# Latent attention with keys on partitions: scores computed transposed, row maxima from the high parts only, fp32 value products in two column halves

## Chip, cores, metric

One Trainium2 chip, one core. The metric is the device time of one execution in microseconds, lower is better; the time before is the median of three runs.

## The reference, cut to what matters

The kernel is one encoder layer: adaLN, an attention mixer with two head groups, an output projection, then a routed mixture of 16 experts. The change is in the first head group, the latent attention (eight heads, 1024 positions, 96 columns of q and k, 64 of v):

```python
def mla_attention(q, k, v):
    B, S, H, Dq = q.shape
    nblk = S // Q_BLOCK
    scale = Dq ** -0.5
    qb = q.reshape(B, nblk, Q_BLOCK, H, Dq).transpose(1, 0, 2, 3, 4)

    def one_block(q_blk):
        s = jnp.einsum('bqhd,bkhd->bhqk', q_blk, k).astype(jnp.float32) * scale
        p = jax.nn.softmax(s, axis=-1).astype(v.dtype)
        return jnp.einsum('bhqk,bkhd->bqhd', p, v)

    o = lax.map(one_block, qb)
    return o.transpose(1, 0, 2, 3, 4).reshape(B, S, H, v.shape[-1])
```

## The kernel before

Everything is fp32. Where a plain fp32 product would be slow the kernel splits an operand into a high part, rounded to the type fp32r, and a low part, the rest (`split`, L82: the cast on ScalarE, the subtraction on VectorE), and adds three fp32r products, high x high, high x low and low x high.

The stages follow each other: adaLN and the input norm; the input projections (the latent q, k and v go to DRAM as `qd`, `kd`, `vd`; `kv_out`, L500, stores v through `vsplit`, L426, already as high and low part); the dilated attention (L668 to L837); the latent attention (L884 to L963); the output projection with the router (L1000 on); the experts (L1425 on). Instructions are placed on each engine's queue by a planner that may move one ahead of another in the text where its inputs and buffers allow it; an engine then works through its queue in order.

In the latent attention `load_head` (L585) brings a head's q, k and v, `prep_head` (L596) transposes 512 positions of q or k on TensorE and splits them. One step of the loop at L937 is one block of 128 queries. `mscore` (L616) puts queries on partitions: six products of 512 columns fill a 128x1024 block `big`, VectorE takes the maximum of each row, and `mexpo` (L640) lets ScalarE compute the exponentials with that maximum as its bias, and their sum. Two steps later `transp` (L898) transposes the exponentials on TensorE, eight blocks of 128x128, and splits them into `pth` and `ptl`. For every two blocks `pv` (L910) adds 16 products: the stationary side holds v's high and low parts beside each other (`k1h`), the moving side is `pth` or `ptl`; two halves of the result are added afterwards. The reciprocals of the sums go to DRAM and come back repeated over 64 partitions (`rows`), and GpSimd multiplies (L929).

The dilated attention has its own `score` (L707), `weights` (L746, a row of reciprocals stored and read back) and `pv` (L760), whose fp32 value products use the two column halves of the array (`tile_position=(0, 64 * e)`); their line is L770. A plain fp32 product shows in the trace as two records.

Of the kernel before, what the change touches and what calls it, by code (L numbers as in the profile page):

```python
# [13 lines left out]
F32 = mybir.dt.float32  # L14
F32R = mybir.dt.float32r
# [27 lines left out]
MS, ME = (1, 2), (2, 3)  # L43

ADV, AV, LATE = (2, 4, 6), 7, 6

KP, XD, WB, TW = 4, (1, 3, 5, 7), 4, 4

# [5 lines left out]
def block_kernel(ctx: ExitStack, tc: tile.TileContext, A: dict, out: bass.AP, dbg=None):  # L54
# [34 lines left out]
    vd = scratch("vd", [S, MH * 2 * VD])  # L89
# [336 lines left out]
    def vsplit(t, src, dst):  # L426

        vv = wk.tile([P, 8, 2, 64], F32R, name="vv")
        split(vv[:, :, 0], vv[:, :, 1], src)
        nc.sync.dma_start(dst[t * P:(t + 1) * P, :], vv.bitcast(F32).rearrange("p h z d -> p (h z d)"))  # L430
# [69 lines left out]
    def kv_out(t, got):  # L500
# [5 lines left out]
        vsplit(t, uv[:, :, ND:], vd)  # L506
# [78 lines left out]
    def load_head(h):  # L585
        e = h % 2
        q = qk_tile(f"k2h{e}", F32, NT * QD).rearrange("p (j c) -> p j c", c=QD)
        k = qk_tile(f"k2l{e}", F32, NT * QD).rearrange("p (j c) -> p j c", c=QD)
        v = qk_tile(f"k1h{e}", F32R, NT * 2 * VD).rearrange("p (j c) -> p j c", c=2 * VD)
        for eng, dst, src, n in ((nc.sync, k, kd, QD), (nc.sync, q, qd, QD), (nc.gpsimd, v, vd, 2 * VD)):  # L590
            eng.dma_start(dst, src[:, h * n:(h + 1) * n].rearrange("(j p) c -> p j c", p=P))
        loads[h] = (q, k, v)
# [3 lines left out]
    def prep_head(h, n, z):  # L596

        q, k, v = loads[h]
        if h not in hs:
            hs[h] = {x: (qk_tile(f"{y}h{h % 2}", F32R), qk_tile(f"{y}l{h % 2}", F32R))  # L600
                     for x, y in (("q", "q1"), ("k", "q2"))}
            hs[h]["v"] = v
# [10 lines left out]
    sc, den, rows, last_exp = {}, {}, {}, [None]  # L613
    drow = scratch("drow", [MH, S])

    def mscore(h, t, early=False):  # L616
        T = hs[h]
        qh, ql = T["q"]
        kh, kl = T["k"]
        qs = slice(t * P, (t + 1) * P)  # L620
        if early:
            ps = [mid(), mid()]
        else:
            b = big()
            ps = [b[:, 0:512], b[:, 512:1024]]
        for a, b_, first, last in ((qh, kh, True, False), (qh, kl, False, False), (ql, kh, False, True)):
            for z in range(2):
                nc.tensor.matmul(ps[z], a[:QD, qs], b_[:QD, z * 512:(z + 1) * 512], start=first, stop=last)  # L628
        if early:
            mx = const.tile([P, 3], F32, name="mxe", bufs=2)  # L630
            for z in range(2):
                nc.vector.tensor_reduce(mx[:, z:z + 1], ps[z], axis=AX.X, op=ALU.max)
# [977 lines left out]
```

## Time and profile before

| what | value |
|---|---|
| median of three runs | 1394.82 us (1392.77 to 1396.35) |
| the profiled execution | 1390.52 us |
| its span | 1388.0 us |
| mean granted TensorE clock | 0.988 of full speed |
| busy: TensorE, VectorE, ScalarE, GpSimd | 95%, 80%, 64%, 14% |

The span goes from the first to the last instruction of the profiled execution, whose own time lies 2.5 us above it; the median of the timed runs is 4.3 us higher. A matmul's record covers its whole way through the array, so records overlap, and the rate is read from the distance of their starts. "x6" behind a shape counts the instructions of a merged row.

### The profile page before, as it was taken

The numbers are of one execution on the slowest core, as the hardware profiler recorded it, in microseconds if no ns is written. First come the engines' busy times: TensorE is split into PE (matmuls) and PEld (weight loads), VectorE is DVE, ScalarE is ACT, GpSimd is POOL, SyncE is SP. The second block draws the span as 40 slices with busy tenths as digits, with TensorE's granted clock in tenths as the row PEclk, the third lists the DMA queues.
The fourth block names the chain that finished last, engine by engine and source line by source line (L and its number), as shares of the span: only waits on it lengthen the run. The fifth ranks groups of instructions, "written<-read, shape, count | busy, mean of one in ns | idle before, by whom it ended". The sixth has DMA issues, their size and how long they took to land.

```text
span 1388.0 us, 21350 instructions
## 1 busy us (share of the span) xinstructions
PE 1324.7 (95%) x7710; PEld 1076.0 (78%) x7710; DVE 1104.5 (80%) x2088; ACT 888.8 (64%) x1421; POOL 191.0 (14%) x230
## 2 busy tenths in 40 slices
PE   4999999999999999999998599999999999999997
PEld 3787788965557999997887478888888888887774
DVE  5764567466657888888477889999999999988887
ACT  5622124255546777777432488888888888878874
POOL 1021011110005101002220121111111111410010
PEclk9999999999999999999999699999999999999999
DMA  9785567254225242112544899999999999999934
GB/s 272 198 284 184 164 230 260 68 153 123 73 57 168 47 80 58 24 24 83 192 166 153 332 345 337 391 393 389 393 391 393 395 390 389 394 364 360 358 105 199
DMA packets 162704, 325.36 MB, mean 234 GB/s; under 512 B 41499, under 2 KB 84571, under 8 KB 162598
## 3 DMA queue, kind: packets, MB, share of 16 engines
q1 hardware_dynamic: 149398, 301.97, 60.5%
q0 software_dynamic: 13200, 22.02, 6.7%
q8 instruction: 60, 0.98, 0.3%
q14 instruction: 46, 0.38, 0.1%
HBM read 286.66 MB, written 37.31 MB: 233 GB/s over the span
## 4 chain that ended last, share of the span: by engine, by line
PE 88%; DVE 6%; ACT 2%; DMA 2%; issue 1%; SPq 0%; DVEq 0%; ACTq 0%
PE big L1354 23%; PE big L1405 12%; PE big L628 6%; PE big L1045 6%; PE mid L916 4%; PE mid L907 4%; PE mid L78 4%; PE mid L80 3%; PE mid L79 3%; PE big L725 2%; PE mid L743 2%; PE mid L1328 2%; PE mid L770 2%; PE big L720 1%; PE big L1369 1%; PE big L78 1%
## 5 line engine op out<-in xcount | busy, mean ns | idle before, releaser
L1314 DVE TENSOR_TENSOR mwl<-mraw,mwh 128x1024 fp32r<-128x1024 f32 x384 | 450.2, 1221 | 28.9 <-ACT mwh L1312 25.3
L1312 ACT CAST mwh<-mraw 128x1024 fp32r<-128x1024 f32 x384 | 391.6, 1062 | 54.1 <-PE big L1354 44.8
L1354 PE MATMUL big<-mwh,xeh 128*128 128x512 f32 x480 | 149.5, 393 | 0.2 <-ACT mwh L1312 0.2
L1354 PE MATMUL big<-mwl,xeh 128*128 128x512 f32 x480 | 149.2, 392 | 0.5 <-DVE mwl L1314 0.5
L1354 PE MATMUL big<-mwh,xel 128*128 128x512 f32 x480 | 147.9, 390 | 0.0
L1354 PEld LDWEIGHTS big<-mwl,xeh 128*128 128x128 f32 x480 | 89.3, 188 | 20.5 <-DVE mwl L1314 2.1
L1354 PEld LDWEIGHTS big<-mwh,xel 128*128 128x128 f32 x480 | 90.0, 188 | 19.1
L1354 PEld LDWEIGHTS big<-mwh,xeh 128*128 128x128 f32 x480 | 88.9, 188 | 19.8 <-ACT xeh L83 0.8
L78 PE MATMUL mid<-wh,hTh 128*128 128x512 f32 (+2 forms) x264 | 94.7, 359 | 0.0
L79 PE MATMUL mid<-wl,hTh 128*128 128x512 f32 (+2 forms) x264 | 93.2, 353 | 0.0
L80 PE MATMUL mid<-wh,hTl 128*128 128x512 f32 (+2 forms) x264 | 93.2, 353 | 0.0
L83 ACT CAST pth<-mid 128x512 fp32r<-128x512 f32 x128 | 68.7, 589 | 34.7 <-PE mid L907 34.2
L84 DVE TENSOR_TENSOR ptl<-mid,pth 128x512 fp32r<-128x512 f32 x128 | 85.3, 682 | 1.0 <-ACT pth L83 0.3
L1321 POOL DMA_INDIRECT xe<-h2d,ix x16 | 37.3, 2333 | 352.9 <-DVE xel L84 330.6
L1405 PE MATMUL big<-mwl,hTh 128*128 128x512 f32 x256 | 80.7, 395 | 2.6 <-DVE mwl L1314 2.5
L1405 PE MATMUL big<-mwh,hTh 128*128 128x512 f32 x256 | 81.4, 398 | 0.4 <-ACT mwh L1312 0.4
L636 DVE TENSOR_REDUCE mx<-big 128x1 f32<-128x1024 f32 x62 | 75.6, 1219 | 6.5 <-PE big L628 6.1
L1405 PE MATMUL big<-mwh,hTl 128*128 128x512 f32 x256 | 79.4, 390 | 0.0
L734 ACT ACTIVATE P<-P,mx 128x512 f32<-128x512 f32 x64 | 45.7, 716 | 43.3 <-DVE mx L730 43.3
L916 PE MATMUL mid<-pth,k1h 128*128 128x256 f32 x256 | 64.9, 292 | 0.5 <-DVE mx L637 0.5
L1334 ACT ACTIVATE xe<-mid,cols 128x128 f32<-128x128 f32 x128 | 48.9, 471 | 21.1 <-PE mid L1328 21.0
L916 PE MATMUL mid<-ptl,k1h 128*128 128x256 f32 x256 | 62.3, 282 | 0.0
(369 smaller groups left out, 2791.1 us busy)
## 6 DMA issues: line engine op xcount, KB each, us to landing
mraw<-in_w_gate_dram SPq DMA_DIRECT2D x64, 1024.0 KB
mraw<-in_w_up_dram SPq DMA_DIRECT2D x63, 1024.0 KB
mraw<-in_w_down_dram SPq DMA_DIRECT2D x63, 1024.0 KB
wada<-in_w_ada_dram SPq DMA_DIRECT2D x48, 512.0 KB
x<-in_x_dram SPq DMA_DIRECT2D x16, 512.0 KB
raw<-in_w_in_dram SPq DMA_DIRECT2D x12, 512.0 KB
vd<-vv SPq DMA_DIRECT2D x8, 512.0 KB
k1h<-vd POOLq DMA_DIRECT2D x8, 512.0 KB, 7.0
```

Of the source, the lines that this page charges most:

```text
L78: nc.tensor.matmul(o, xh, wh, start=start, stop=False, **kw)
L79: nc.tensor.matmul(o, xh, wl, start=False, stop=False, **kw)
L80: nc.tensor.matmul(o, xl, wh, start=False, stop=stop, **kw)
L84: return nc.vector.tensor_tensor(l, src, h.bitcast(F32), op=ALU.subtract)
L628: nc.tensor.matmul(ps[z], a[:QD, qs], b_[:QD, z * 512:(z + 1) * 512], start=first, stop=last)
L636: nc.vector.tensor_reduce(mx[:, 0:1], b, axis=AX.X, op=ALU.max)
L916: nc.tensor.matmul(op[:, 0:256], V[:, k], pt[:, k], start=(k == 0 and i == 0), stop=(k == NT - 1 and i == 1))
L1045: lastmm[0] = nc.tensor.matmul(ps[z], a[k], w[k][:, z * 512:(z + 1) * 512], start=(first and i == 0), stop=(last and i == KT - 1))
L1312: high[0] = nc.scalar.copy(h[j], raw[:, j])
L1314: low[0] = nc.vector.tensor_tensor(l[j], raw[:, j], h[j].bitcast(F32), op=ALU.subtract)
L1354: nc.tensor.matmul(o[:, zs], a[:, k], w[i][j][:, zs], start=(k == 0 and a is xh and i == 0), stop=(k == KT - 1 and a is xl))
L1405: nc.tensor.matmul(yp[:, zs], a[:, k], w[i][j][:, zs], start=(k == 0 and a is th and i == 0), stop=(k == KT - 1 and a is tl))
```

## The change

- `vout` takes the place of `vsplit`: v is stored in fp32, once, so `vd` and its load are half as large. `load_head` loads only q and k, into one buffer each (`k2h0`, `k2l0`); v is loaded by a function of its own.
- `maxpass`: for a block of 128 queries, the product of the high parts alone, over all keys, and its row maxima on VectorE. `maxrow`: one product brings the negated maxima of four blocks to four partitions, and VectorE writes them, each in its own block's columns and zero elsewhere, as rows 96 to 99 of the high part of q; the same rows of the high part of k hold ones.
- `score`: keys are on partitions now. 128 keys by 512 queries in three products; the first has 100 rows of contraction, so the maxima are subtracted in it. ScalarE's exponential goes straight from PSUM to a ring of 13 buffers. Nothing is transposed after it.
- `accum` adds the exponentials of the key blocks on VectorE; `dens` sums over partitions with eight fp32 products against a column of ones; `denrow` transposes the reciprocals, stores them and reads them back repeated.
- `pv`: for each block of 128 keys two fp32 products, 512 queries each, one in each column half. They run one head behind the scores, one key block in every second step (in each step of the last head's first half; its own follow in the second half).
- PSUM pools are closed and opened again around the stage (`big` two, `mid` three, one `op`).

The loop is a step of 512 queries by 128 keys, sixteen to a head. The core of the diff:

```diff
     def load_head(h):
-        e = h % 2
-        q = qk_tile(f"k2h{e}", F32, NT * QD).rearrange("p (j c) -> p j c", c=QD)
-        k = qk_tile(f"k2l{e}", F32, NT * QD).rearrange("p (j c) -> p j c", c=QD)
-        v = qk_tile(f"k1h{e}", F32R, NT * 2 * VD).rearrange("p (j c) -> p j c", c=2 * VD)
...
+        q, k = (qk_tile(n, F32, NT * QD).rearrange("p (j c) -> p j c", c=QD) for n in ("k2h0", "k2l0"))
...
+    def maxpass(h, z, u):
+
+        qh, kh = hs[h]["q"][0], hs[h]["k"][0]
+        ps = big()
+        for zz in range(2):
+            nc.tensor.matmul(ps[:, zz * 512:zz * 512 + 512], qh[:QD, (4 * z + u) * P:(4 * z + u + 1) * P], kh[:QD, zz * 512:zz * 512 + 512],
+                             start=True, stop=True)
+        if u == 0:
+            mxs[h, z] = const.tile([P, 4], F32, name="mxg", bufs=2)
+        nc.vector.tensor_reduce(mxs[h, z][:, u:u + 1], ps, axis=AX.X, op=ALU.max)
...
+        def maxrow(h, z):
+
+            nm = nms[z]
+            nc.vector.tensor_scalar(nm[:, own4], mxs.pop((h, z)), -1.0, None, op0=ALU.mult)
+            ps = mid()
+            nc.tensor.matmul(ps[:QD + 4, 0:P], nm, identr, start=True, stop=True)
+            nc.vector.tensor_tensor(hs[h]["q"][0][own4, z * 512:z * 512 + 512].rearrange("p (u c) -> p u c", c=P),
+                                    ps[own4, None, 0:P].to_broadcast([4, 4, P]), dmask[own4], op=ALU.mult)
+
+        def score(h, z, k):
+
+            (qh, ql), (kh, kl) = hs[h]["q"], hs[h]["k"]
+            zs, ks = slice(z * 512, z * 512 + 512), slice(k * P, k * P + P)
+            ps = mid()
+            nc.tensor.matmul(ps, kh[:QD + 4, ks], qh[:QD + 4, zs], start=True, stop=False)
+            nc.tensor.matmul(ps, kh[:QD, ks], ql[:QD, zs], start=False, stop=False)
+            nc.tensor.matmul(ps, kl[:QD, ks], qh[:QD, zs], start=False, stop=True)
...
+            last_exp[0] = nc.scalar.activation(pt[h, z, k // 2][:, k % 2], ps, AF.Exp, scale=scale)
+
+        def accum(h, z, u):
+
+            if u == 1:
+                acc[h, z] = wk.tile([P, 2, 512], F32, name="acc", bufs=2)
+            a = acc[h, z]
+            nc.vector.tensor_tensor(a, pt[h, z, 0] if u == 1 else a, pt[h, z, u], op=ALU.add)
+            if u == 3:
+                nc.vector.tensor_tensor(a[:, 0], a[:, 0], a[:, 1], op=ALU.add)
+
+        def dens(h):
+
+            ps = mid()
+            for z in range(2):
+                a = acc.pop((h, z))
+                for u in range(4):
+                    nc.tensor.matmul(ps[:, 4 * z + u:4 * z + u + 1], a[:, 0, u * P:(u + 1) * P], ones[:, 0:1],
+                                     start=True, stop=True, skip_group_check=True)
+            D8[h] = wk.tile([P, 8], F32, name="D8")
+            nc.vector.reciprocal(D8[h], ps[:, 0:8])
...
+        def pv(h, k):
+
+            if k == 0:
+                ops[h] = psum.tile([P, 512], F32, name="op", bufs=1)
+            for z in range(2):
+                nc.tensor.matmul(ops[h][64 * z:64 * z + 64], hs[h]["v"][:, k], pt[h, z, k // 2][:, k % 2], start=(k == 0),
+                                 stop=(k == NT - 1), tile_position=(0, 64 * z), skip_group_check=True)
...
+                    nc.vector.tensor_tensor(mixM[hp // 2][64 * e:64 * e + 64, hp % 2, z * 512:z * 512 + 512], o[zs], a[zs],
+                                            op=ALU.mult)
...
+        for h in range(MH):
+            last = h == MH - 1
+            load_v(h)
+            for i in range(16):
+                z, k = divmod(i, 8)
+                score(h, z, k)
+                if k % 2 and k > 1:
+                    accum(h, z, k // 2)
+                nh, nz = (h, 1) if z == 0 else (h + 1, 0)
+                if nh < MH:
+                    if k in (0, 1, 3, 4):
+                        maxpass(nh, nz, (0, 1, 3, 4).index(k))
+                    if k == 6:
+                        maxrow(nh, nz)
+                if not last and i in (1, 3, 5, 12):
+                    prep_head(h + 1, "kkqq"[(1, 3, 5, 12).index(i)], (0, 1, 0, 1)[(1, 3, 5, 12).index(i)])
+                if i == 13 and h + 2 < MH:
+                    load_head(h + 2)
...
+                if h:
+                    if i == 2:
+                        dens(h - 1)
+                    if i == (3 if last else 5):
+                        denrow(h - 1)
+                    if last and z == 0:
+                        pv(h - 1, k)
+                    if not last and i % 2:
+                        pv(h - 1, i // 2)
...
+                if last and z and k >= 2:
+                    pv(h, k - 2)
+        dens(h)
+        pv(h, NT - 2)
+        denrow(h)
+        pv(h, NT - 1)
```

`load_head(1)` and `maxrow(0, 0)` stand before the loop, and the four `maxpass` of head 0's first half at the end of the dilated stage, where the first two score blocks were. Removed are `mscore`, `mexpo`, `transp`, the old `pv` and `vsplit`.

## Rows read from the trace of the kernel before

**Rows 1.** The page, busy time and share of the span by engine.
```profile
PE 1324.7 (95%) x7710; PEld 1076.0 (78%) x7710; DVE 1104.5 (80%) x2088; ACT 888.8 (64%) x1421; POOL 191.0 (14%) x230
```

**Rows 2.** Windows: length, busy PE, PEld, DVE, ACT, POOL, clock, DMA share, GB/s.
```profile
200.00:300.00 100.00, 99.78 (x630) 85.93 (x628) 61.47 (x194) 41.15 (x104) 14.86 (x40) 1.00 0.54 172
...
440.00:620.00 180.00, 180.00 (x1262) 163.97 (x1261) 156.88 (x270) 138.55 (x263) 28.73 (x16) 1.00 0.27 53
```

**Rows 3.** The chain of waits, in order of time: start, length, what.
```profile
449.90 1.39 PE big L628 x6
451.28 0.88 PE mid L907 x8
...
454.43 1.91 PE mid L916 x16
...
458.59 0.44 PE mid L606 x4
```

**Rows 4.** The score line: shortest, median, longest record in ns, first and last start.
```profile
L628 PE MATMUL big<-q2h,q1h x124: 389/398/500, 422.1 to 634.4; 96*128 96x512 f32 x124
```

**Rows 5.** TensorE in order of time around a column-split group (several narrow windows).
```profile
416.94 0.28 PE L770 MATMUL mid<-pt,q2l 128*64 128x128 f32 x2
...
417.15 0.50 PE L628 MATMUL mid<-q2h,q1h 96*128 96x512 f32 x1
...
417.15 0.73 PE L628 MATMUL mid<-q2h,q1h 96*128 96x512 f32 x2
...
418.42 0.39 PE L628 MATMUL mid<-q2h,q1l 96*128 96x512 f32 x1
...
418.74 0.33 PE L770 MATMUL mid<-pt,q1l 128*64 128x128 f32 x2
...
419.00 0.60 PE L770 MATMUL mid<-pt,q1l 128*64 128x256 f32 x4
...
418.74 1.95 PE L770 MATMUL mid<-pt,q1l 128*64 128x128 f32 x20
```

**Rows 6.** TensorE in order of time where the router's fp32 products end.
```profile
666.13 0.82 PE L1088 MATMUL mid<-wr,x1T 128*128 128x16 f32 x6
666.80 0.70 PE L1045 MATMUL big<-woh,mixh 128*128 128x512 f32 x2
```

**Rows 7.** Groups of VectorE and ScalarE instructions, 420 to 646 us, last the page's.
```profile
L84 DVE TENSOR_TENSOR ptl<-mid,pth 128x512 fp32r<-128x512 f32 x128 | 85.3, 682 | 1.0 <-ACT pth L83 0.3
L636 DVE TENSOR_REDUCE mx<-big 128x1 f32<-128x1024 f32 x62 | 75.6, 1219 | 6.5 <-PE big L628 6.1
L83 ACT CAST pth<-mid 128x512 fp32r<-128x512 f32 x128 | 68.7, 589 | 34.7 <-PE mid L907 34.2
...
L647 ACT ACTIVATE k1l<-mid,mxe 128x512 f32<-128x512 f32 x4 | 2.7, 683 | 8.0 <-DVE mxe L637 8.0
...
L1314 DVE TENSOR_TENSOR mwl<-mraw,mwh 128x1024 fp32r<-128x1024 f32 x384 | 450.2, 1221 | 28.9 <-ACT mwh L1312 25.3
```

**Rows 8.** VectorE and GpSimd in order of time, 422 to 435 us.
```profile
422.22 0.15 DVE L648 TENSOR_TENSOR dene<-dene,mxe 128x1 f32<-128x1 f32 x1
...
425.37 2.35 DVE L648 TENSOR_TENSOR dene<-dene,mxe 128x1 f32<-128x1 f32 x1
...
425.35 9.33 POOL L892 TENSOR_TENSOR wo<-wo,gta 128x1024 f32<-128x1024 f32 x4 [20.20 <-ACT pth L83]
```

**Rows 9.** The two ends: a window (columns as in rows 2), TensorE in order.
```profile
420.00:440.00 20.00, 17.92 (x106) 14.96 (x103) 16.62 (x29) 13.01 (x27) 9.86 (x5) 0.91 0.59 201
...
641.66 0.73 PE L1045 MATMUL big<-woh,mixh 128*128 128x512 f32 x2 [0.71 <-ACT woh L83]
...
645.89 0.39 PE L1045 MATMUL big<-woh,mixl 128*128 128x512 f32 x1
```

**Rows 10.** The chain of waits around a stored and broadcast row of reciprocals.
```profile
406.69 2.16 DMA arow<-row
...
409.49 4.53 DMA A<-arow
```

More of the change, by code (lines that the diff above doesn't have):

```diff
@@ L601, in prep_head @@
                      for x, y in (("q", "q1"), ("k", "q2"))}
-            hs[h]["v"] = v
+            kh = hs[h]["k"][0]
+            nc.scalar.copy(kh[QD:QD + 4], ones[QD:QD + 4, 0:1].to_broadcast([4, S]))
         src = q if n == "q" else k
@@ L612, in block_kernel @@
     scale = QD ** -0.5
[L613 to L632, printed above, removed]
-            nc.vector.tensor_tensor(mx[:, 0:1], mx[:, 0:1], mx[:, 1:2], op=ALU.max)
-        else:
-            mx = wk.tile([P, 2], F32, name="mx", bufs=4)
-            nc.vector.tensor_reduce(mx[:, 0:1], b, axis=AX.X, op=ALU.max)
-        nc.vector.tensor_scalar(mx[:, 1:2], mx[:, 0:1], -scale, None, op0=ALU.mult)
-        sc[h, t] = (ps if early else b, mx)
@@ L910, in pv @@
-        def pv(h, u):
-            ph, pl = pts.pop((h, u))
-            V = hs[h]["v"]
-            op = mid()
-            for k in range(NT):
-                for i, pt in enumerate((ph, pl)):
-                    nc.tensor.matmul(op[:, 0:256], V[:, k], pt[:, k], start=(k == 0 and i == 0),
-                                     stop=(k == NT - 1 and i == 1))
-            hp, e = divmod(h, 2)
-            own = slice(64 * e, 64 * e + 64)
-            oth = slice(64 - 64 * e, 128 - 64 * e)
-            o2 = wk.tile([P, 256], F32, name="o2", bufs=1)
-            nc.scalar.copy(o2[own], op[oth, 0:256])
-            nc.vector.tensor_tensor(mixM[hp // 2][own, hp % 2, u * 256:(u + 1) * 256], op[own, 0:256], o2[own],
-                                    op=ALU.add)
-            n = 2 if h == MH - 1 else 4
-            if (u + 1) % n == 0:
-                cs = slice((u + 1 - n) * 256, (u + 1) * 256)
-                m = mixM[hp // 2][own, hp % 2, cs]
-                nc.gpsimd.tensor_tensor(m, m, rows[h][own, cs], op=ALU.mult)
+        identr = wk.tile([P, P], F32R, name="identr", bufs=1)
@@ new lines, in denrow @@
+        def denrow(h):
+            tp = mid()
+            nc.tensor.transpose(tp[0:8, 0:P], D8.pop(h), ident)
+            row = wk.tile([8, P], F32, name="row8", bufs=1)
+            nc.scalar.copy(row, tp[0:8, 0:P])
+            nc.sync.dma_start(drow[h], row)
+            a = A8[h] = wk.tile([P, 512], F32, name="A8", bufs=1)
+            for z in range(2):
+                src = drow[h, 4 * z:4 * z + 4]
+                nc.sync.dma_start(a[64 * z:64 * z + 64], bass.AP(tensor=src.tensor, offset=src.offset, ap=[[0, 64], [1, 512]]))
@@ L966, in block_kernel, with mid @@
+        dens(h)
+        pv(h, NT - 2)
+        denrow(h)
+        pv(h, NT - 1)
+        with tc.issue_after(last_exp[0].ins):
+            mix0 = mix_half(mp, 0, mixD, nc.vector)
+            for i in range(NW):
+                split_wo(mp, korder[i])
+    sps.close()
+    sps = ExitStack()
+    psum = pool(sps, "psumo", space=PSUM)
+    def mid():
+        return psum.tile([P, 512], F32, name="mid", bufs=4)
     sqk.close()
```

128 lines of the change are left out of this document (49 added, 79 removed).

## Prediction

> **What bounds the kernel now.** I read the page first, for the shares of the engines: TensorE (PE) is busy for 95% of the span, VectorE for 80%, ScalarE for 64% [rows 1]. A share over 1388 us hides the stages, so next came the table of windows over the stage that the change rewrites. From 440 to 620 us TensorE has no idle time at all, at full clock, while VectorE works 157 of 180 us and ScalarE 139 [rows 2]. So in this stage time is TensorE's time, and work taken from the others pays nothing by itself. The chain of waits, in order of time, shows a stage with only TensorE pieces in it: two score blocks of 1.39 us, two groups of eight transposes of 0.88 us, one group of sixteen value products of 1.91 us, and 0.44 us for four transposes of the next head's q or k [rows 3]. The list of the score line gives the period: 62 blocks, 124 records, start between 422.1 and 634.4 us, thus 61 steps of 3.48 us, and 27.8 us for a head of eight [rows 4]. The pieces alone give 4 x (2 x 1.39 + 2 x 0.88 + 1.91) + 4 x 0.44 = 27.6 us, so almost nothing is left unexplained.
>
> **What goes.** Per head 8 x 0.88 = 7.0 us of transposed exponentials and 4 x 1.91 = 7.6 us of value products leave TensorE. ScalarE loses the casts and VectorE the subtractions on those transposes (128 each, 0.59 and 0.68 us [rows 7]); GpSimd loses the eight multiplications by 1/denominator. All of these run beside a full TensorE, so only TensorE's part counts.
>
> **What comes, on TensorE, per head.** Scores: still 48 products of 512 columns at 1.39/6 = 0.232 us, so 11.1 us as before. That they now have 100 rows of contraction, not 96, I cost at nothing: a record of 96 rows [rows 4] and one of 128 [rows 9] both last 0.39 us. High-part products for the maxima: 16 x 0.232 = 3.7 us, all new. Denominators: eight fp32 products against a column of ones. The router's products, two records each for one fp32 product, are the nearest: six records from 666.13 to 666.80, 0.112 us each [rows 6]; 16 x 0.112 + 0.08 for the return to fp32r (the next two fp32r records take 0.70 us, where a distance of 0.23 and a length of 0.39 make 0.62) = 1.9 us. The next head's transposes now stand alone between other products: 4 x (0.44 + 0.08) = 2.1 us. The two products that turn the maxima into rows, and the transpose of the denominators, are 0.11 to 0.2 us each: 0.4 us.
>
> The value products decide. They become full fp32, 128x64 stationary, 512 moving columns, in two column halves of the array. The dilated stage has this form with fewer columns. Twenty records (ten fp32 products, two passes each) take 1.95 us; with 128 columns a pair of records comes every 0.11 us, with 256 columns the second pair follows after 0.22 us (four records in 0.60 us, where one lasts 0.38) [rows 5]. Both halves therefore run at the same time, and 512 columns are 0.43 us a pass, 0.86 us for both halves of one key block: 8 x 0.86 = 6.9 us a head, less than the 7.6 of now. But going into and out of this form costs time, which the same rows show. In: last score record at 418.42, first column record at 418.74, 0.32 us and not 0.23; and the first pair lasts 0.33, not 0.28. Out: last pair at 416.94, next score record at 417.15, 0.21 us and not 0.11; its record lasts 0.50, not 0.40, so that two take 0.73 and not 0.62 (0.23 + 0.39). In all 0.09 + 0.05 + 0.10 + 0.11 = 0.35 us an excursion. Before, a value group is entered 32 times in an unsplit form; after it is entered 64 times (8 heads x 8 key blocks), each time with a pair of products between scores. So 0.86 + 0.35 = 1.21, and 9.7 us a head.
>
> The Trainium skill, TensorEngine Tiling (Array Packing), section Theoretical Speedup, promises up to 2x for a stationary side of 64 columns, and under Key Properties says that a change of tiling mode drains the engine. By the first alone the values would cost 6.9 us a head and the stage would gain; the trace agrees with both, and prices the drain at 0.35 us.
>
> Sum per head: 11.1 + 3.7 + 9.7 + 1.9 + 2.1 + 0.4 = 28.9 us against 27.8. Over eight heads **+8 us**.
>
> **VectorE.** Per head: maxima 8 x 1.22 = 9.8; sums of exponentials 6 x 1.22 + 2 x 0.68 = 8.7 (no addition of this form is there; a subtraction from SBUF of 128x1024 took 1.22, one of 512 columns 0.68 [rows 7]); low parts 2.7; max rows 2 x (0.14 + 0.68) = 1.6; the last multiplication 1.4; reciprocal 0.2. That is 24.4 of 28.9 us, 84%, against 87% now, where TensorE never waits. ScalarE: 16 exponentials of 0.68, casts 2.4, row of ones about 1.1, one copy: about 15 us, half of the head. Neither becomes the bound in a steady head. In head 0 it is otherwise, since TensorE has no value products yet. In its first half VectorE has 4 x 1.22 + 3 x 1.22 + 0.68 + 3 x 0.68 + 0.82 = 12.1 us, TensorE 8 x 0.695 + 4 x 0.46 + 3 x 0.52 + 0.1 = 9.1, and the second half's scores stand behind the max row: 3 us lost. GpSimd adds to it. While its four multiplications of the output weights ran (9.33 us), an addition of one column on VectorE took 2.35 us, where the same form took 0.15 before them [rows 8]. Both inputs of the new sums are in SBUF; three of them meet GpSimd here, each may wait 0 to 2.2 us, and I take 1 in all because the maxima go first. In the second half the value products of head 0 can be drawn forward. Head 0: **+4 us** (0 to 10). The Trainium skill, SBUF — State Buffer, section Who interferes with whom, has this as an exclusive lock between GpSimd and a VectorE instruction with two SBUF inputs; by that the wait would be up to a whole GpSimd operation, which the 2.35 us agrees with.
>
> **The two ends.** At the start, 420 to 440 us, TensorE now stands idle 2.1 us and has a mean clock of 0.91 [rows 9], 3.8 us in all. After, the first score must wait for four maxima, 4 x 1.22 us behind the first product, and a max row: about 423.7 us, with 4.8 us of work at hand from 417.15 (four maxima products, the last dilated group of 1.95, two transposes of head 1). I let the one replace the other: 0 (-3.8 to +4). At the end, now, the first product of the out projection waits 0.71 us for a split weight [rows 9], and two later ones as long. After, head 7 is scaled only when its whole denominator is back: exponential 0.7, sums 1.9, denominators and copies 2.6, store and broadcast 7.3 (406.69 to 414.02 in the dilated stage, [rows 10]), multiplication 1.4, split 1.2: 15 us. TensorE has in that time three value steps and the denominators (5.5) and 36 projection products (8.3), 13.8. So **+1 us** (-2 to +5).
>
> **Costed at nothing.** v is stored once instead of as two parts: one ScalarE cast less, one VectorE copy for a subtraction, eight times, beside a projection stage in which TensorE is 99.8% busy from 200 to 300 us [rows 2]. Without that cover it would be a gain of 5 us. On SP's queue the denominator's broadcast waits for its store; behind it stands the next head's load, eight steps (14 us) later against 7.3. q and k have one buffer now, loaded at step 13 and read at step 1 of the next head, 7 us later; late loads would stop all products behind that transpose (0 to 1 us a head). GpSimd's v load halves and lies a head ahead.
>
> **Sum.** 8 + 4 + 1 = +13 us on the profiled execution: 1390.5 to 1403.5. The three timed runs have their median 4.3 us higher, at 1394.8, so I predict **1408 us**; the stages behind have TensorE in the chain too and pass the delay on whole. What can be told from no change is 0.3%, 4.2 us.
>
> **Rivals.**
> - The switches are not paid, because value steps are laid next to each other or the drain hides. For it: the order in the trace isn't that of the text everywhere, products of the out projection run among the last value products [rows 9]. Against: the crossings that the rows hold are paid in both directions. Price: 64 x 0.35 = 22 us off, 1408 - 22 = 1386. It decides once 49 of the 64 are saved (17 us): faster. 0.18.
> - No change: some 25 to 49 saved, or head 0 and the start hidden (-4, -3.8) with a few saved besides: about 1396. 0.17.
> - The max row becomes a wait. The product that turns the maxima stands two steps behind the last of them on TensorE, and VectorE, in order, still has a sum of 1.22 and a low part of 0.68 ahead: all scores and value products queue behind it. At 0.7 us for each of 16 halves +11 us, at twice that +22: 1419 to 1430. Against: VectorE now works 87% and no such wait shows. 0.13.
> - My forecast, TensorE's own sum, +5 to +21 us, thus 1400 to 1416: 0.52.
>
> Faster 0.18, same 0.17, slower 0.13 + 0.52 = 0.65. The range takes in the first rival's side of the bound and most of the third: 1387 to 1425.
>
> **What would show it.** Right: in the steady heads TensorE has no idle time, a period of about 28.9 us, column pairs 0.43 us apart with some 0.2 us of gap on each side; head 0 has waits on VectorE. Wrong: value steps standing in runs; waits at the max-row product; periods below 27.8; or sums of exponentials much longer than 1.22 us.

## Result, and the profile after

The changed kernel takes 1445.43 us (median of four executions, 1445.18 to 1447.31) against 1395.59 before on the same chip (four, 1392.77 to 1397.15): a ratio of 1.0362, interval 1.0343 to 1.0382. The forecast was 1408, from 1387 to 1425. The direction is right, the time lies outside the range: I added 13 us where there are 50. The profiled execution has a span of 1443.5 us, 55.5 more than before.

The page's busy line for the changed kernel, beside [rows 1]:

```profile
PE 1374.3 (95%) x7222; PEld 1022.6 (71%) x7222; DVE 1105.3 (77%) x1973; ACT 818.6 (57%) x1265; POOL 173.5 (12%) x221
```

TensorE has 488 instructions fewer and is busy 50 us longer, at the same share. So the loss is TensorE time, as forecast, but four times as much. Part of it is the granted clock, with a mean of 0.976 where the kernel before has 0.988.

Where it lies is read from four marks in each trace: the start of the last dilated value product, of the first full score, of the last latent value product, and of the first expert product. Before they stand at 420.4, 417.2, 645.8 and 791.4 us, after at 420.1, 428.7, 688.2 and 845.6. The start thus costs 11.8 us more (from the first mark to the second -3.3 before, +8.5 after), scores and values 31.0 (228.6 before, 259.6 after), the stretch up to the experts 11.7 (145.7 and 157.4). The rest of the span differs by 1.3 us, what lies ahead by -0.3.

**The steady heads.** The score line of the changed kernel, as in [rows 4]; 16 of its 128 records make a head:

```profile
L884 PE MATMUL mid<-q1h,q2h x128: 393/477/796, 428.7 to 684.0; 100*128 100x512 f32 x128
```

The distance between the first scores of two heads is 29.3, 27.4, 32.5, 34.7, 33.1, 34.6 and 34.7 us, not 28.9. TensorE in order of time shows why (start, length, line, shape; the last two columns of a line count its records):

```profile
520.45 0.64 PE L934 MATMUL op<-kn,k1h 128*64 128x512 f32 x1
520.45 0.64 PE L934 MATMUL op<-pt,k1h 128*64 128x512 f32 x1
520.93 0.59 PE L934 MATMUL op<-kn,k1h 128*64 128x512 f32 x1
520.93 0.59 PE L934 MATMUL op<-pt,k1h 128*64 128x512 f32 x1
521.46 0.50 PE L884 MATMUL mid<-q1h,q2h 100*128 100x512 f32 x1
...
523.39 0.95 PE L908 MATMUL mid<-ones,acc 128*128 128x1 f32 x8
524.20 0.47 PE L619 MATMUL big<-q2h,q1h 96*128 96x512 f32 x1
524.60 1.86 PE L934 MATMUL op<-kn,k1h 128*64 128x512 f32 x2
...
532.04 1.07 PE L934 MATMUL op<-k2h,k1h 128*64 128x512 f32 x2
533.04 0.27 PE L916 MATMUL mid<-ident,D 128*8 128x128 f32 x1
533.25 0.64 PE L934 MATMUL op<-pt,k1h 128*64 128x512 f32 x1
```

At 520.45 both halves of a key block run as forecast: two records begin together, two more 0.48 us later, and scores go on after 1.01. At 532.04 one half stands alone. It takes as long, 1.00 us up to the next instruction, and its partner comes after a transpose and pays again. The planner, to which the halves are two independent products, has parted them: the trace holds 83 runs of value products, 36 with both halves of a block (median 1.01 us up to the next instruction), 44 with one half alone (1.00 us) and three of two blocks. The lone half at 524.60 takes 1.86 us, with the granted clock at 0.5 (1.2 GHz) from 524.75 on, right behind the eight narrow products for the denominators (two groups of four, each of eight records; the second is shown). Such stretches make 21.0 us of the stage, against 3.4 before.

**Head 0.** Windows, columns as in [rows 2]; the first answers to [rows 9]:

```profile
420.00:440.00 20.00, 14.55 (x55) 9.61 (x52) 15.63 (x18) 5.65 (x10) 9.84 (x5) 0.81 0.66 214
440.00:460.00 20.00, 18.51 (x71) 10.54 (x70) 19.78 (x19) 8.26 (x14) 11.47 (x4) 0.93 0.22 76
440.00:620.00 180.00, 178.48 (x697) 96.33 (x695) 132.49 (x148) 71.49 (x122) 15.04 (x8) 0.96 0.16 44
```

VectorE is full in the second window. Four of its instructions in order of time, and GpSimd's two groups of multiplications of the output weights:

```profile
434.56 3.34 DVE L898 TENSOR_TENSOR acc<-k1l,k1l 128x1024 f32<-128x1024 f32 x1 [0.93 <-ACT k1l L891]
...
441.29 1.73 DVE L873 TENSOR_SCALAR nm<-mxg 128x4 fp32r<-128x4 f32 x1
...
447.58 1.64 DVE L900 TENSOR_TENSOR acc<-acc 128x512 f32<-128x512 f32 x1
...
450.27 2.28 DVE L898 TENSOR_TENSOR acc<-k2h,k2l 128x1024 f32<-128x1024 f32 x1
```

```profile
427.44 9.38 POOL L855 TENSOR_TENSOR wo<-wo,gta 128x1024 f32<-128x1024 f32 x4 [19.73 <-DMA wo<-in_w_out_dram]
439.54 11.93 POOL L855 TENSOR_TENSOR wo<-wo,gta 128x1024 f32<-128x1024 f32 x4 [2.71 <-DMA wo<-in_w_out_dram]
```

Beside GpSimd the sum of 1024 columns takes 3.34 and 2.28 us, elsewhere 1.21; that of 512 columns 1.64, elsewhere 0.68. The 3.34 end 1.08 us behind GpSimd's first group, about the sum's own length: it looks as if it had begun only then.

**The start.** TensorE, then VectorE, in order of time:

```profile
422.38 0.73 PE L619 MATMUL big<-q2h,q1h 96*128 96x512 f32 x2 [0.85 <-DVE mxg L623]
...
426.53 0.43 PE L875 MATMUL mid<-identr,nm 128*100 128x128 f32 x1 [1.15 <-DVE nm L873]
...
428.68 0.63 PE L884 MATMUL mid<-q1h,q2h 100*128 100x512 f32 x1
```

```profile
421.10 3.49 DVE L623 TENSOR_REDUCE mxg<-big 128x1 f32<-128x1024 f32 x3 [1.32 <-PE big L619]
424.51 1.05 DVE L751 TENSOR_TENSOR mraw<-mid,A 128x512 f32<-128x512 f32 x1
425.41 0.20 DVE L860 CAST identr<-ident 128x128 fp32r<-128x128 f32 x1
```

Between the maxima and the first score VectorE also does the last dilated normalization and prepares constants, and TensorE waits for each maximum. Before, full scores ran from 417.15 among the dilated products [rows 5].

**The end.** TensorE and VectorE where the output projection begins:

```profile
690.23 0.70 PE L1081 MATMUL big<-woh,mixh 128*128 128x512 f32 x2
...
695.01 0.82 PE L1081 MATMUL big<-woh,mixh 128*128 128x512 f32 x2
700.37 1.22 PE L1081 MATMUL big<-wo,mixh 128*128 128x512 f32 x2 [4.55 <-DVE wo L84]
```

```profile
696.71 0.68 DVE L943 TENSOR_TENSOR mraw<-op,A 64x512 f32<-64x512 f32 x1 [4.42 <-DMA A<-drow]
...
699.09 2.89 DVE L84 TENSOR_TENSOR wo<-wo,woh 128x1024 fp32r<-128x1024 f32 x2
```

Head 7's scaling waits for its stored and broadcast row, and the next split of the output weights stands behind it in VectorE's order. So TensorE has 14 projection products (690.23 to 695.4), and then nothing for 4.6 us.

### The profile page after: what moved, and what is told of

Same layout as the page of the kernel before. It is cut to its first block, busy times and chain, and to the rows that moved or that the text cites. A ratio compares the mean times of both kernels' runs of the same rounds, so it can differ in the third digit from the quotient of the medians.

```text
span 1443.5 us, 20114 instructions
## 1 busy us (share of the span) xinstructions
PE 1374.3 (95%) x7222; PEld 1022.6 (71%) x7222; DVE 1105.3 (77%) x1973; ACT 818.6 (57%) x1265; POOL 173.5 (12%) x221
## 4 chain that ended last, share of the span: by engine, by line
PE 86%; DVE 7%; DMA 3%; ACT 2%; issue 1%; SPq 0%; POOL 0%; DVEq 0%; ACTq 0%; POOLq 0%
PE big L1390 22%; PE big L1441 12%; PE op L934 6%; PE big L1081 5%; PE mid L884 3%; PE mid L78 3%; PE mid L80 3%; PE mid L79 3%; PE big L685 2%; PE mid L703 2%; PE mid L730 2%; PE big L619 2%; PE mid L886 2%; PE mid L885 2%; PE mid L1364 2%; PE big L680 1%
## 5 line engine op out<-in xcount | busy, mean ns | idle before, releaser
L623 DVE TENSOR_REDUCE mxg<-big 128x1 f32<-128x1024 f32 x64 | 77.8, 1221 | 33.0 <-PE big L619 31.9
L891 ACT ACTIVATE pt<-mid 128x512 f32<-128x512 f32 x68 | 40.6, 597 | 75.3 <-PE mid L886 73.7
L1357 POOL DMA_INDIRECT xe<-h2d,ix x16 | 31.5, 1971 | 359.9 <-DVE xel L84 337.6
L934 PE MATMUL op<-pt,k1h 128*64 128x512 f32 x136 | 63.1, 619 | 0.0
L884 PE MATMUL mid<-q1h,q2h 100*128 100x512 f32 x128 | 60.1, 470 | 2.0 <-DVE q2l L84 1.9
L884 PEld LDWEIGHTS mid<-q1h,q2h 100*128 100x128 f32 x128 | 25.0, 195 | 48.1 <-issue 17.3
```

What stands on the lines that cost most here:

```text
L623: nc.vector.tensor_reduce(mxs[h, z][:, u:u + 1], ps, axis=AX.X, op=ALU.max)
L884: nc.tensor.matmul(ps, kh[:QD + 4, ks], qh[:QD + 4, zs], start=True, stop=False)
L934: nc.tensor.matmul(ops[h][64 * z:64 * z + 64], hs[h]["v"][:, k], pt[h, z, k // 2][:, k % 2], start=(k == 0), stop=(k == NT - 1), tile_posi ...
```

## Experiments

All ratios are to the kernel before, run on the same chip (its medians there: 1390.0 to 1393.6, and 1395.6 beside the changed kernel). The chips differ from group to group, so medians of different groups are compared by their ratios. "Stage" is from the first full score to the last latent value product, "end" from there to the first expert product, in the profiled execution; "half" is the time at a granted clock of 0.5 within the stage.

| run | median us | ratio (interval) | stage | end | half |
|---|---|---|---|---|---|
| before | | 1 | 228.6 | 145.7 | 3.4 |
| changed | 1445.4 | 1.0362 (1.0343 to 1.0382) | 259.6 | 157.4 | 21.0 |
| e1_tied | 1425.0 | 1.0235 (1.0192 to 1.0278) | 243.0 | 154.8 | 31.4 |
| e2_textorder | 1439.7 | 1.0340 (1.0296 to 1.0385) | 262.1 | 154.1 | 43.7 |
| e3_apart | 1491.9 | 1.0716 (1.0671 to 1.0760) | 308.3 | 155.4 | 32.0 |
| e4_dencol | 1427.8 | 1.0255 (1.0189 to 1.0321) | 246.1 | 152.7 | 36.6 |
| e5_two | 1421.8 | 1.0210 (1.0176 to 1.0244) | 243.1 | 153.7 | 35.8 |
| e6_wolater | 1439.5 | 1.0345 (1.0314 to 1.0376) | 255.5 | 154.9 | 40.4 |
| e7_two_wolater | 1411.8 | 1.0169 (1.0108 to 1.0229) | 231.1 | 154.7 | 13.9 |
| e9_tail | 1414.9 | 1.0184 (1.0122 to 1.0247) | 229.7 | 152.0 | 12.9 |
| e8_sums | 1417.1 | 1.0191 (1.0144 to 1.0239) | 229.7 | 154.4 | 13.0 |
| e10_nomax | 1391.8 | 0.9994 (0.9974 to 1.0013) | 215.7 | 152.6 | 31.4 |
| e11_sums_tail | 1412.1 | 1.0124 (1.0086 to 1.0161) | 239.9 | 150.7 | 26.3 |
| e13_after_dve | 1436.0 | 1.0334 (1.0305 to 1.0363) | 251.8 | 157.4 | 13.8 |
| e12_dve | 1412.1 | 1.0152 (1.0122 to 1.0181) | 228.7 | 154.1 | 10.8 |
| e14_four | 1407.0 | 1.0110 (1.0086 to 1.0133) | 228.3 | 151.9 | 13.6 |

### Where the two halves stand: e1, e2, e3

In e1 both halves of a block are issued behind the other TensorE work of their step (`step` collects it):

```diff
-            for z in range(2):
-                nc.tensor.matmul(ops[h][64 * z:64 * z + 64], ...
+            with ExitStack() as tied:
+                for m in step:
+                    tied.enter_context(tc.issue_after(m.ins))
+                for z in range(2):
+                    nc.tensor.matmul(ops[h][64 * z:64 * z + 64], ...
```

> The two column halves of each value step are made to follow each other: they may only be issued behind the other TensorE work of their step, so the planner can no longer put scores between them. The changed kernel has 83 runs of value records (44 of a lone half); this one has 61 and no lone half. Theory A (a lone half costs as much as a pair, 0.86 us of passes and 0.35 us of switching): 22 runs x 1.21 = 27 us less, about 1418 us (1414 to 1424). Theory B (the lone halves only filled time in which TensorE would have waited for VectorE or for a score buffer): under 5 us less, 1440 or more. Theory C (the half-clock stretches, 23.9 us of them in the stage, are the loss): they stay, 1435 or more.

e2 goes further: each TensorE instruction of the loop behind the one before it in the text.

```diff
-        T[0] = nc.tensor.matmul(*a, **k)
+        with tc.issue_after(T[0].ins):
+            T[0] = nc.tensor.matmul(*a, **k)
```

> All TensorE instructions of the stage's loop are issued in the order of the text; the other engines stay free. 64 runs of value records, no lone half. Theory A: as with the tied halves, 1418 within 4 us, since TensorE stays the bound. Theory B (TensorE in fixed order waits at the max-row product for VectorE, 0.7 to 1.4 us in each half): 11 us or more above the tied kernel.

e3 puts the scores of a step between the two halves, so that nearly every half stands alone.

```diff
+                    m0 = half(h - 1, due, 0, before_)
+                    with tc.issue_after(m0.ins):
+                        score(h, z, k)
...
-                        pv(h - 1, i // 2)
+                        half(h - 1, due, 1, step)
```

> The opposite: in heads 0 to 6 one half of each value step is put ahead of its step's scores and the other behind them. 113 runs of value records where the changed kernel has 83. Theory A: 30 x 1.21 = 36 us more than the changed kernel, about 1481 us (1470 to 1490). Theory B: the order of the halves matters little, 1440 to 1452. Theory C: no more half clock than now, so within 5 us of the changed kernel.

e1 takes 20 us off the changed kernel in the medians (by the ratios 0.0127, some 18 us), e3 puts 46 on. With 61, 83 and 113 runs of value products the time goes one way with their number. From 83 to 61 the stage loses 16.6 us although e1 has 10.4 us more at half clock (worth about half of that, 5.2, where TensorE is the bound): 21.8 / 22 = 1.0 us a run. From 83 to 113, reckoned in the same way, it is 43.2 / 30 = 1.4, more than a run costs by itself. In e1 an excursion, in order of time, is this:

```profile
531.78 0.39 PE L596 MATMUL mid<-q1h,q2l 96*128 96x512 f32 x1
532.10 0.64 PE L949 MATMUL op<-k2h,k1h 128*64 128x512 f32 x1
532.10 0.64 PE L949 MATMUL op<-pt,k1h 128*64 128x512 f32 x1
532.58 0.59 PE L949 MATMUL op<-k2h,k1h 128*64 128x512 f32 x1
...
533.11 0.50 PE L596 MATMUL big<-q2h,q1h 96*128 96x512 f32 x1
533.45 0.39 PE L596 MATMUL mid<-q1h,q2h 100*128 100x512 f32 x1
```

In: 0.32 us from the last score record, not 0.23. First pass 0.48, not 0.43. Out: 0.53 after the second pass, not 0.43, and 0.34 up to the next record, not 0.23. Together 0.09 + 0.05 + 0.10 + 0.11 = 0.35 us, the forecast's price. e1's heads without a stretch at half clock last 28.6 us, the forecast's 28.9. e2, with 64 runs, gives 15 of the 20 us back: TensorE then waits in an order that doesn't give way to late maxima, 15 times and 12.8 us in all for their rows (e1: 3 times, 4.5 us), and 43.7 us of its stage are at half clock. So what e1 gains is not order as such, but both halves at once.

The Trainium skill's page TensorEngine Tiling (Array Packing) has both halves of this: up to 2x for at most 64 columns (Theoretical Speedup), and a drain at each change of the tiling mode (Key Properties). The traces agree with the drain at 0.35 us; of the 2x nothing is had by a half that stands alone, 1.00 us against 1.01 for both.

### Denominators without narrow products: e4, e8

e4 is e1 with one column-split product of ones[128x64] with the sums, and VectorE's reciprocal of the whole 128x512:

```diff
-                    nc.tensor.matmul(ps[:, 4 * z + u:4 * z + u + 1], a[:, 0, u * P:(u + 1) * P], ones[:, 0:1], ...
...
-            nc.vector.reciprocal(D8[h], ps[:, 0:8])
...
+                nc.tensor.matmul(ps[64 * z:64 * z + 64], ones[:, 0:64], a[:, 0], ..., tile_position=(0, 64 * z))
...
+            nc.vector.reciprocal(A8[h], ps)
```

> As with the tied halves, and the denominators come from one fp32 product per column half with a stationary block of ones, 64 columns wide: the sums appear already repeated on 64 partitions, VectorE takes the reciprocal of 128x512, and the eight narrow products, the transpose, the stored row and its broadcast go. By their sum alone (16 x 0.112 + 0.08 + 0.2 = 2.1 us against 0.86 to 1.21 us a head) 8 to 10 us below the tied kernel; theory C (the narrow products bring the half clock: four of the six drops inside the loop follow them, 1.7 us each) 7 us more; the wait for the broadcast at the end goes, some 4 us. Together about 1400 us; without theory C about 1406.

No gain: the group list shows what I had not priced.

```profile
L925 DVE RECIPROCAL A<-mid 128x512 f32<-128x512 f32 x8 | 26.8, 3348 | 0.0
```

VectorE spends 3.35 us on it, the rows of maxima come later, and TensorE waits for them ten times, 11.2 us in all (e1: 4.5). e8 (on e7, below) keeps the sums as a product, but sends them through memory as 8x128 to be inverted:

```diff
+            a = A8[h] = wk.tile([P, 512], F32, name="A8", bufs=1)
+            nc.scalar.copy(a, ps)
...
+                nc.sync.dma_start(srow[h, 4 * z:4 * z + 4], a[64 * z:64 * z + 1].rearrange("a (u p) -> a u p", p=P))
...
+            nc.sync.dma_start(d, srow[h])
+            nc.vector.reciprocal(d, d)
...
```

> As e7_two_wolater, but heads 0 to 6 have no narrow products: the sums become two column-split products with ones, are stored, read back as 8x128, inverted in 8x128, stored and broadcast. Theory N (the narrow products cost TensorE 1.9 us per head, against about 1.2 for the column-split sums, and the granted clock falls behind them, 1.7 us each of the three times in e7_two_wolater): 5 + 4 less than e7_two_wolater's 1412, so 1403 (1399 to 1407), without half-clock stretches in heads 1 to 6. Rival (the clock falls in the waits for the row of maxima): the half-clock stretches stay, 1406 to 1411.

1417.1 (1410.6 to 1423.8): missed. In its trace heads 3, 5 and 6 last 27.5 us without a stretch at half clock, 2.5 less than in e7 (of which 1.7 are its stretches at half clock), which is the theory. But head 4 lasts 36.0 and head 2 30.9, both with GpSimd's multiplications in them, and there the clock falls with a wait. So the fall comes with narrow products (e1, e7) and with waits (e4, e8) alike; in undisturbed heads without narrow products none shows. Nor does each head with narrow products have one: in the changed kernel four of the seven heads that hold them.

### More key blocks in an excursion: e5

```diff
-                    if not last and i % 2:
-                        pv(h - 1, i // 2)
+                    if not last and i % 4 == 3:
+                        pv(h - 1, i // 2 - 1, i // 2)
```

> As e1_tied, but the value products of two key blocks stand side by side: 32 runs of value products where e1_tied has 61. Theory A (each excursion into and out of the column-split form costs TensorE about 0.35 us by itself, however many products stand in it): 29 excursions fewer, 10 us less than e1_tied's 1425, so 1415 (1411 to 1418). Theory B (the price lies in the products themselves; what remains over the kernel before is head 0 and half-clock stretches): no change, 1422 to 1428.

1421.8, so at most 3 of the 10 us, which the intervals don't tell from none; the stage is as long as e1's. The excursion with two blocks costs no more than that with one, but new waits take the saving, here at the row of maxima:

```profile
550.47 0.27 PE L877 MATMUL mid<-identr,nm 128*100 128x128 f32 x1 [0.51 <-DVE nm L875]
```

Heads without a stretch at half clock last 28.3 us (28.6 in e1), and windows of 20 us in which e1's TensorE is full have 19.35 to 19.86. A stretch of 17.07 us at half clock begins at 460.21, among waits of 1.47 and 1.16 us at the end of head 0, and head 1 lasts 34.9 us where e1's has 30.4. The third rival of the forecast appears, once TensorE has less to do.

### GpSimd and VectorE: e6, e7, e13, e12

e6 is e1 with GpSimd's multiplications behind the value loads of heads 2 and 4 in its order, four behind each; e7 is e5 with the same.

```diff
...
+            with tc.issue_after(vload[0].ins):
                 nc.gpsimd.tensor_tensor(w, w, gta, op=ALU.mult)
```

> As e1_tied, but GpSimd multiplies w_out by the gate behind the value load of head 2, no longer in head 0. Theory H (in head 0 VectorE is the bound, and GpSimd's two multiplications there hold up its operations with two inputs in SBUF by about 6 us, which lets TensorE wait and its granted clock fall): 5 to 10 us less than e1_tied's 1425, so 1415 to 1420, and operations of head 0 at their usual durations. Rival (head 0 is bound by the reductions of the maxima alone, whatever GpSimd does, or the delay comes back in heads 2 to 4, where the multiplications then lie): 1422 to 1427.

> The edits of e5_two and e6_wolater together on e1_tied. If excursions and head 0 are separate costs, both savings add: 1425 - 10 - 7 = 1408 (1403 to 1412). If TensorE is no longer the bound once the excursions are halved (VectorE busy 15 to 18 of 20 us in steady heads, or waits for maxima and exponentials that bring stretches at half clock), the second saving is lost: 1413 to 1418.

In e6 head 0 falls from 30.5 to 23.3 us, as theory H has it, and yet the kernel is 14 us slower than e1: heads 2 and 4, where the multiplications now lie, last 40.5 and 40.0. The delay came back, and larger. e7 comes out at 1411.8, near the sum of both savings, but its executions are spread from 1408.2 to 1423.9. What happens in such a head is plainest in e10 (below), in order of time, GpSimd, VectorE and TensorE:

```profile
468.02 9.26 POOL L859 TENSOR_TENSOR wo<-wo,gta 128x1024 f32<-128x1024 f32 x4
468.18 9.65 DVE L904 TENSOR_TENSOR acc<-acc 128x512 f32<-128x512 f32 x1
...
477.89 1.87 PE L912 MATMUL mid<-ones,acc 128*128 128x1 f32 x8 [7.55 <-DVE acc L904]
```

A sum of 512 columns, 0.68 us elsewhere, has both inputs in SBUF and lasts until GpSimd's four multiplications are done; the denominators wait for it, and all of TensorE behind them. The Trainium skill's page SBUF — State Buffer, section Who interferes with whom, says that such an instruction contends with a GpSimd instruction that reads SBUF. The trace agrees, and shows the wait run over four GpSimd instructions in a row. It isn't always so. In e7's profiled execution the same sum gets in between them, GpSimd takes longer instead, and head 2 lasts 28.9 us:

```profile
479.71 10.83 POOL L860 TENSOR_TENSOR wo<-wo,gta 128x1024 f32<-128x1024 f32 x4
480.33 2.32 DVE L905 TENSOR_TENSOR acc<-acc 128x512 f32<-128x512 f32 x1
```

e13 is the changed kernel itself with these multiplications on VectorE, two in each of heads 1 to 4, e12 is e5 with the same:

```diff
-            nc.gpsimd.tensor_tensor(w, w, gta, op=ALU.mult)
+            nc.vector.tensor_tensor(w, w, gta, op=ALU.mult)
...
-                if h in (2, 4) and i % 4 == 3:
-                    load_wo(korder[(h - 2) * 2 + i // 4])
+                if 1 <= h <= 4 and i % 8 == 7:
+                    load_wo(korder[(h - 1) * 2 + i // 8])
```

> The changed kernel, with w_out multiplied by the gate on VectorE, one tile in each half of heads 1 to 4, and not on GpSimd in head 0. Theory G (GpSimd's multiplications hold VectorE up in head 0, and TensorE waits there): 7 us less than 1445, as head 0 became 7 us shorter in e6_wolater, so 1438 (1434 to 1441), and VectorE's operations of head 0 at their usual durations. Rival (head 0 is bound by VectorE's own work, and its eight multiplications of about 1.2 us come on top): 1444 to 1450.

> As e5_two (halves tied, two key blocks in one excursion), with w_out multiplied on VectorE as in e13_after_dve. Theory G: head 0 as short as in e7_two_wolater (22 to 23 us) and no delay in heads 2 to 4; e7_two_wolater's quicker executions, 1408, less up to 3 us: 1403 to 1408, and the executions within 5 us of each other, where e7_two_wolater's are spread over 16. Rival (the spread and the delay have another cause): 1408 to 1424, spread as before.

e13: 1436.0, 9.4 less than the changed kernel in the medians; but the kernel before is 5.6 us quicker on this chip too, and the ratios, 1.0334 and 1.0362, have intervals that overlap. What the edit does is read from the trace: head 0 lasts 23.9 us, not 29.3, and the stage is 7.8 us shorter. Two instructions of head 0 named above, in e13's order of time, and its window:

```profile
434.30 1.23 DVE L898 TENSOR_TENSOR acc<-k1l,k1l 128x1024 f32<-128x1024 f32 x1 [0.76 <-ACT k1l L891]
...
438.91 0.15 DVE L873 TENSOR_SCALAR nm<-mxg 128x4 fp32r<-128x4 f32 x1
...
440.00:460.00 20.00, 19.94 (x97) 12.96 (x96) 17.48 (x21) 9.92 (x17) 0.00 (x0) 1.00 0.21 72
```

VectorE has eight multiplications of 1.2 us more, the first of them in head 0, and the sums there are back at 1.2 and 0.7 us. The 2.4 us of the stage beyond head 0 needn't be GpSimd: e13 also has 79 runs of value products for 83 and 7.2 us less at half clock. e12, at 1412.1 (1409.5 to 1415.4), misses its range by 4 us, but its spread over four executions is 6 us where e7's is 16, and its stage lasts 228.7 us: as long as before.

### The maxima: e10

e7 without products, reductions and rows of the maxima:

```diff
-                        maxpass(nh, nz, (0, 1, 3, 4).index(k))
...
-                        maxrow(nh, nz)
...
-    scale = QD ** -0.5
+    scale = 0.05 * QD ** -0.5
```

> As e7_two_wolater, but all that serves the maxima is left out (their products, reductions, rows), the four extra rows hold zeros, and the exponential's scale is smaller so that nothing overflows; the output is not the reference's. Theory M (the start, where the first score stands 8 us behind the last dilated product, and what head 0 has over its TensorE work, about 5 us, are the maxima on VectorE): 8 heads x 3.9 us of TensorE work + 8 + 5 less than e7_two_wolater's 1412, so 1368 (1362 to 1373), the first score within 2 us of the last dilated product. Rival (the start is bound by the preparation of the first keys and queries, maxima are hidden beside it): only the TensorE work goes, 1379 to 1383, and the first score stays where it is.

1391.8, and not 1368: heads 2 and 4, with GpSimd's multiplications in them, last 34.4 and 34.3 us, heads 3, 5 and 6 23.8, 4 less than the 27.9 of e7's head 1. The two delays are 21 us; without them the run would stand at 1371 (an estimate), inside theory M's range. At the start the first score comes at 423.9, where e7 has 428.0. It is the half of what theory M had, since another wait is next; VectorE's side of it stands below TensorE's:

```profile
423.86 0.77 PE L888 MATMUL mid<-q1h,q2h 100*128 100x512 f32 x1 [4.53 <-DVE mraw L754]
422.65 1.06 DVE L754 TENSOR_TENSOR mraw<-mid,A 128x512 f32<-128x512 f32 x1 [5.68 <-DMA A<-arow]
```

The first score waits until the last dilated group is scaled, as the PSUM pools are opened again there, and the scaling waits for its stored and broadcast row. Of e7's 8.5 us between the last dilated value product and the first score 4.8 are left in e10, 4.53 of them this wait; 3.7 were the maxima.

### The end, and the quickest version: e9, e11, e14

e9 is e7, e11 is e8, with the last head's denominators as in e4 (`dencol(h)` for `dens(h)` and `denrow(h)`).

> As e7_two_wolater, but the last head's denominators are a column-split product of ones with the sums and one reciprocal of 128x512 (3.35 us) in place of narrow products, a stored row and its broadcast. Theory T (the 6 us in which TensorE waits ahead of the output projection are the row's way through memory): 4 to 7 us less than e7_two_wolater. Rival (VectorE's splits of w_out stand behind that multiplication and end last anyway): within 2 us of e7_two_wolater.

> e8_sums with the last head's denominators as in e9_tail (a column-split product and one reciprocal of 128x512). If the ends add up, 3 us (as far as the first router product stood earlier in e9_tail's trace) less than e8_sums. Against the kernel before: still slower, 1397 to 1406, if head 0's start (8 us) and the maxima's TensorE work (3.9 us per head) are what is left of the loss; equal or faster only if the half-clock stretches go altogether.

The end is 2.7 us shorter in e9 and 3.7 in e11 than in the runs they are made from, half of theory T; the 5.64 us that TensorE waits for a split weight in e7 become two shorter waits on the same splits (first e7's, then e9's):

```profile
668.70 1.22 PE L1090 MATMUL big<-wo,mixh 128*128 128x512 f32 x2 [5.64 <-DVE wo L84]
...
662.15 0.73 PE L1099 MATMUL big<-wo,mixh 128*128 128x512 f32 x2 [1.10 <-DVE wo L84]
...
665.64 0.73 PE L1099 MATMUL big<-wo,mixh 128*128 128x512 f32 x2 [1.82 <-DVE wo L84]
```

In the medians the 3 us can't be told from the spread (e9 1414.9 against e7's 1411.8), and e11 misses its range with 1412.1: in its trace heads 2 and 4 last 37 us, again with GpSimd's multiplications in them. e14 joins everything: e11, the multiplications on VectorE, and four key blocks in an excursion, 18 runs of value products.

```diff
-                    if not last and i % 4 == 3:
-                        pv(h - 1, i // 2 - 1, i // 2)
+                    if not last and i in (7, 11):
+                        pv(h - 1, *range(i - 7, i - 3))
```

> e11_sums_tail with w_out multiplied on VectorE, and the value products of four key blocks in one excursion (19 runs of value products). If an excursion costs 0.4 us whatever stands in it, half of them save 0.8 us per head, 6 in all; with the 8 to 10 us of each of the two delays in heads 3 and 5 gone from e11_sums_tail's profiled 1417: 1391 to 1398, within 0.5% of the kernel before. Rival (rows of maxima and exponentials behind the longer blocks of value products end later and TensorE waits): 1400 to 1408.

1407.0, the lowest median of the versions that leave nothing out (e11's interval overlaps), still 1.1% slower than before; its rival held. Its heads 3 to 6 last 28.0 us without a stretch at half clock, and no longer by TensorE's work alone: it waits 16 times, 11.1 us in all, for the rows of maxima, though only about 0.9 us in each of heads 4 to 6. Two of its windows:

```profile
440.00:460.00 20.00, 18.72 (x82) 12.51 (x80) 19.77 (x23) 12.78 (x22) 0.00 (x0) 1.00 0.26 80
...
560.00:580.00 20.00, 18.94 (x86) 11.56 (x86) 19.62 (x24) 10.91 (x18) 0.88 (x1) 1.00 0.21 54
```

VectorE has 19.6 to 19.8 us of 20 in these two, and 16.1 and 16.0 in the windows on either side of the second. e8, with two blocks in an excursion, has the same heads in 27.5 us, so four blocks made them longer. Counted from start to start in one undisturbed head each, the value products take 8.1 us in e1, 7.4 in e8 and 7.2 in e14, the products of the maxima with what they wait for 4.1, 5.1 and 5.6: what the excursions save is lost there, beside VectorE's chain of maxima. e10's 23.8 us a head don't show VectorE as the bound: they are 4.1 less than e7's head 1, and its expectation had 3.9 of that as TensorE's own work.

## Why the prediction was wrong

- **TensorE is the bound, and only its part counts:** right for the changed kernel, whose steady windows have TensorE full, VectorE at 13 to 16 of 20.
- **The price of an excursion, 0.35 us, and the sum of 28.9 us a head:** right, by e1's rows and its heads of 28.6.
- **"64 excursions, each time with a pair of products between scores":** this is the step that failed, the largest single one; the two ends below were mis-sized besides. The text writes the halves one behind the other, and I took that for the order on TensorE, though the forecast itself says that the trace's order isn't the text's everywhere. There are 83 runs, 44 of them of a single half, which fill the array by half and pay as much. Tying them gives 16.6 us of the stage and, by the ratios, some 18 us of the time back (e1). My first rival had the planner join steps; it parted them.
- **Head 0, +4 with 1 us for GpSimd:** the mechanism was there, with the row that shows it [rows 8], its size was off. I bounded a wait by that row's 2.2 us and took 1 in all; e10 shows 9 for one. Without GpSimd's work head 0 of the changed kernel falls from 29.3 to 23.9 us (e13).
- **Start, 0:** +11.8. My chain had the first score at 423.7; it comes at 428.7. I left out the last dilated scaling, 1.05 us, and the constants, 0.94, which stand in VectorE's order between the maxima and their row, and the full scores that before fill TensorE from 417.15 on. Even without any maxima the first score would come at 423.9, behind that scaling (e10).
- **End, +1:** +11.7. I had 36 projection products to cover 15 us of waiting; 14 could run, since the splits of the output weights queue behind the very multiplication that waits. TensorE then idles 4.55 us at once. Stretches at half clock are 37.5 us here, 23.9 before; only 10.2 of them lie in the projection, at 692 and 699 us, and are worth 5.1 us at most, since the others, as before, stand where TensorE is less than half busy.
- **Account:** of the stage's 31.0 us, 16.6 go with the parted halves (e1) and 7.8 in e13, 5.4 of them in head 0; what is left, 6.6, stands where the forecast has +8 for the heads. 6.6 + 16.6 + 7.8 + 11.8 + 11.7 + 1.0 for the rest make the 55.5. The two shares of the stage come from one edit each, and their clocks differ, so the split is an estimate. The lower mean clock is inside these shares and not beside them; it would be 18 us of the 55.5 if TensorE were the bound everywhere. e12, with both edits and gathered blocks, has the stage at 228.7 and so leaves only the two ends.
- **Rival of the waiting row of maxima, 0.13:** not in the changed kernel, whose TensorE waits for that row 0.2 us in all behind the first score, but the next wait behind its bound (e4, e5, e14).

Open: why the clock falls behind the narrow products of some heads and not of others; and why e7's and e8's executions differ by 13 to 16 us is only argued, from the two courses that a sum beside GpSimd's multiplications takes, 2.32 us in e7's trace and 9.25 to 9.65 in e8's and e10's. With GpSimd out (e12) the spread is 6 us.

## What to carry to other kernels

Products that share the array must also be tied in the order of issue: a planner that sees two independent products may part them, here 44 times, and a half alone cost what both cost. Before work is put on GpSimd, look at what VectorE does next to it in time, not in the text, and price a wait by the whole group's length, not by one instruction's. And a cheaper bound engine is worth only the distance to the next wait: here from 28.6 us a head in e1 to 27.5 in e8, and 28.0 in e14 with still fewer excursions.

## What the hardware showed unexpectedly

- A lone column half of 512 columns takes TensorE 1.00 us up to the next instruction, both halves side by side 1.01 (medians of the changed kernel).
- VectorE's reciprocal of 128x512 takes 3.35 us, 4.9 times its sum of two SBUF tiles of that size (0.68); of 128x8, 0.21.
- One VectorE sum with both inputs in SBUF waited through four GpSimd multiplications in a row: 9.65 us for 0.68 (e10). The same sum took 2.32 us beside such a group in e7.
- The granted clock fell to 0.5 (1.2 GHz) with no idle time of TensorE in the 10 us before, behind eight fp32 products with a single moving column (at 525, 593 and 627 us in the changed kernel; in heads 2, 4 and 7 it stayed at 1.0 behind the same products).
